# Where the two parts of each matmul operand lie in SBUF: offsets and shared tiles in a two-layer decoder trunk

## Chip, core and metric

The kernel runs on one core of a Trainium2 chip. The metric is the device time of one execution in microseconds (us). TensorE does the matrix products, VectorE (DVE) and ScalarE (ACT) the elementwise work, GpSimd (POOL) a few small things; SP issues nearly all DMAs. SBUF is the on-chip memory of 128 partitions; an "address" below is a byte offset inside a partition, the same for all of them. PSUM holds the sums of the matmuls.

## The reference

Two layers over 256 tokens of width 1024, all in float32:

```
for l in range(2):
    x = x + 0.5 * swiglu(rmsnorm(x), ffn1_w_in[l], ffn1_w_out[l])      # 1024 -> 2 x 2816 -> 1024
    h = rmsnorm(x)
    hq, hf, hi, hg, aq, ak, av, ga, gb = split(h @ w_in[l])            # 1024 -> 10752
    y_a = hgrn2(hq, hf, hi, hg) @ w_branch_a[l]                        # gated recurrence, 8 heads
    y_b = dilated_attention(aq, ak, av) @ w_branch_b[l]                # 3 groups of 4 heads, 512 -> 1024
    x = x + (sigmoid(ga) * y_a + sigmoid(gb) * y_b) @ w_out[l]
    x = x + 0.5 * swiglu(rmsnorm(x), ffn2_w_in[l], ffn2_w_out[l])
```

## The kernel before

**Precision.** Every float32 operand of the big products is split into two float32r parts: "hi", a rounded copy, and "lo", the rest. A product is then three matmuls: hi x hi, hi x lo and lo x hi. For weights ACT makes hi (a Copy, L195 or L241) and DVE makes lo (a subtraction, L196 or L242). Activations are split in the same way where they are made: `xh`/`xl` (the normed x, in `norm_parts`), `hh`/`hl` (the hidden layer of SwiGLU), `ph`/`pl` (first the recurrence's output `oah`/`oal`, later the merged branches `mgh`/`mgl`, both in the same two buffers), and `obh`/`obl` (the attention's output). Each of these eight is a tile of its own before the change.

**Two forms of product.** A matmul has a standing operand (128 columns, loaded into the array by a weight load ahead of it) and a moving operand (streamed through).

- `full` and `mm_feat` (L209 to L211): the weights stand, 256 tokens of activations move. Used for both halves of SwiGLU's first product, for SwiGLU's second product except the very last one, for hf, hq, the gates, and the products with w_branch_a, w_branch_b and w_out.
- `wide` and `mm_half` (L219 to L221): 128 tokens of activations stand, 512 columns of weights move. Used for hi, hg, aq, ak, av and for the last product of the kernel, which writes the output.

The three matmuls of the first form, for each row tile k of 128 rows and each 128 columns of weights:

```
nc.tensor.matmul(o, hi[:, f], ah[:, k0 + k, :], start=s, ...)
nc.tensor.matmul(o, hi[:, f], al[:, k0 + k, :], ...)
nc.tensor.matmul(o, lo[:, f], ah[:, k0 + k, :], ..., stop=e)
```

In the profile `mm<-xh,whi` names the output tile, then the inputs.

**Weights.** A unit is up to eight row tiles of 256 columns (1 MB). SP loads it into one of three `raw` buffers; ACT and DVE convert it in half units of four row tiles into `whi` and `wlo`, four buffers each. ACT and DVE work their queues in order, so a conversion that waits for a free buffer holds up what is queued behind it there.

**Addresses.** The tile framework lays out its pools one after the other: the constants (with `xT`, `xh`, `xl`), then `wts` (`raw`, `whi`, `wlo`), and behind it the pools that come and go: `ffn` with `hh`/`hl`; `mix` with `ph`/`pl` and `mg`, and inside it `hgrn` or `attn`. Sizes are rounded to 32 bytes. One row tile of a weight part takes 1024 bytes in a partition, so does one row tile of an activation part, and a step of 128 columns is 512 bytes.

**Order.** The order of instructions on each engine is planned by the framework from the program's order, the tiles' dependences and a model of time (`schedule_with_timeline_sim=True`). It fills the recurrence's and the attention's small float32 matmuls in between the large products. No order is written out by hand around the change, except for `HEAD_ORDER` inside the attention.

Of the kernel before, what the change touches and what calls it, by code (L numbers as in the profile page):

```python
# [31 lines left out]
HEADS = 8  # L32
EPS = 1e-6
# [4 lines left out]
# columns of the constant table  # L38
# [9 lines left out]
def _shape_constants():  # L48
    """Identity, rotary tables and 0/1 or additive masks: functions of the shapes alone."""
    c = np.zeros((128, C_END), np.float32)  # L50
    c[:, C_ID:C_ID + 128] = np.eye(128, dtype=np.float32)
    inv = (10000.0 ** (-np.arange(0, 128, 2) / 128.0)).astype(np.float32)
    ang = np.arange(T, dtype=np.float32)[:, None] * inv[None, :]
    cos, sin = np.cos(ang.astype(np.float64)), np.sin(ang.astype(np.float64))
    for h in range(2):
        r = slice(h * 128, (h + 1) * 128)
        c[:, C_COS + h * 128:C_COS + (h + 1) * 128] = np.concatenate([cos[r], cos[r]], 1)
        c[:, C_SIN + h * 128:C_SIN + (h + 1) * 128] = np.concatenate([-sin[r], sin[r]], 1)
    for h, base, n in ((0, C_M0, 128), (1, C_M1, 256)):
        t = np.arange(128)[:, None] + 128 * h  # L60
        s = np.arange(n)[None, :]
        for g, (w, d) in enumerate(((128, 1), (512, 4), (2048, 16))):
            ok = (t - s >= 0) & (t - s <= w) & ((t - s) % d == 0)
            c[:, base + g * n:base + (g + 1) * n] = np.where(ok, 0.0, -BIG)
    s = (np.arange(128) % 32)[:, None]
    t = np.arange(32)[None, :]
    lv = [(s // 4 == t // 4) & (t - s == d) for d in range(4)]
    lv += [(s // 16 == t // 16) & (t // 4 - s // 4 == d) for d in range(1, 4)]
    lv += [(s < 16) & (t >= 16)]
    for i, m in enumerate(lv):  # L70
        c[:, C_LV + i * 32:C_LV + (i + 1) * 32] = m
    return c
# [3 lines left out]
def trunk(ctx, tc, x, ffn1_norm, ffn1_w_in, ffn1_w_out, mix_norm, w_in, lb_logits, out_norm,  # L76
# [13 lines left out]
    xT = const.tile([128, KD, T], F32, name="xT")  # L90
    xh = const.tile([128, KD, T], F32R, name="xh")
    xl = const.tile([128, KD, T], F32R, name="xl")
# [90 lines left out]
    def unit(w, r0, nk, col, step=0):  # L183
        raw = wts.tile([128, KD, CU], F32, name="raw", bufs=RB)
        for a in range(0, nk, step or nk):
            n = min(step or nk, nk - a)
            nc.sync.dma_start(raw[:, a:a + n, :], w[r0 + a * 128:r0 + (a + n) * 128, col:col + CU].rearrange(
                "(k p) c -> p k c", p=128))
        parts = []
        for a in range(0, nk, step or KH):  # L190
            n = min(step or KH, nk - a)
            hi = wts.tile([128, KH, CU], F32R, name="whi", bufs=WB)
            lo = wts.tile([128, KH, CU], F32R, name="wlo", bufs=WB)
            r = raw[:, a:a + n, :]
            nc.scalar.activation(hi[:, :n, :], r, AF.Copy)  # L195
            nc.vector.tensor_sub(lo[:, :n, :], r, hi[:, :n, :].bitcast(F32))  # L196
            parts += [(hi[:, k, :], lo[:, k, :]) for k in range(n)]
        return parts

    def mm_feat(ps, wu, ah, al, k0, nk, first, last):  # L200
        """ps[feature, fb, token] += W^T a"""
        for k in range(nk):
            hi, lo = wu[k]
            for fb in range(2):
# [3 lines left out]
                e = last and k == nk - 1  # L208
                nc.tensor.matmul(o, hi[:, f], ah[:, k0 + k, :], start=s, stop=False, skip_group_check=True)  # L209
                nc.tensor.matmul(o, hi[:, f], al[:, k0 + k, :], start=False, stop=False, skip_group_check=True)  # L210
                nc.tensor.matmul(o, lo[:, f], ah[:, k0 + k, :], start=False, stop=e, skip_group_check=True)  # L211

    def mm_half(o, h, wu, ah, al, k0, nk, first, last):
        """o[token of half h, column] += a^T W"""
# [8 lines left out]
    def full(w, col, ah, al, nk=KD, step=0):  # L223
        wu = unit(w, 0, nk, col, step)
        ps = ps_mm.tile([128, 512], F32, name="mm")
        mm_feat(ps, wu, ah, al, 0, nk, True, True)
        return ps

    def wide(w, col, ah, al, nk=KD):
        """ps[half][token, column] = a^T W for 512 columns"""  # L230
        ps = [ps_mm.tile([128, 512], F32, name="mm") for _ in range(2)]
        for k0 in range(0, nk, 4):
# [4 lines left out]
            for a in range(0, n, 2):  # L237
                hi = wts.tile([128, KH, CU], F32R, name="whi", bufs=WB).rearrange("p (k a) c -> p k (a c)", a=2)
                lo = wts.tile([128, KH, CU], F32R, name="wlo", bufs=WB).rearrange("p (k a) c -> p k (a c)", a=2)
# [52 lines left out]
    def ffn(l, gi, w1, w2, to_out, x0=None):  # L292
        norm_parts(gi, l)
        with ExitStack() as es:
            fp = es.enter_context(tc.tile_pool(name="ffn", bufs=2))
            hh = fp.tile([128, KF, T], F32R, name="hh", bufs=1)
            hl = fp.tile([128, KF, T], F32R, name="hl", bufs=1)
            xt = None
            for j in range(DFF // CU):
                pa = full(w1, j * CU, xh, xl, step=0 if j or l or gi else FIRST)  # L300
# [8 lines left out]
                pb = full(w1, DFF + j * CU, xh, xl)  # L309
# [15 lines left out]
            if to_out:  # L325
                for c in range(D // CW):
                    ps = wide(w2, c * CW, hh, hl, KF)
# [5 lines left out]
            else:  # L333
                for c in range(D // CU):
                    ps = ps_mm.tile([128, 512], F32, name="mm")
                    k0 = 0
                    for nk in (8, 8, 6):
                        wu = unit(w2, k0 * 128, nk, c * CU)
                        mm_feat(ps, wu, hh, hl, k0, nk, k0 == 0, k0 + nk == KF)
# [5 lines left out]
    def hgrn_pair(wp, st, l, u, pf, vg):  # L345
        W, X, ATs = st
        w = w_in[l]
        if pf is None:
            pf = full(w, MIX_HF + u * CU, xh, xl)
# [9 lines left out]
        pq = full(w, MIX_HQ + u * CU, xh, xl)  # L359
# [8 lines left out]
        if u % 2 == 0:  # L368
            pv = wide(w, MIX_HI + u * CU, xh, xl)
# [8 lines left out]
        def variants(Y, s0, B, m):  # L378
            """Y slot s0 holds queries decayed to the start of their m-block; the next slots
            carry them over one, two and three more m-blocks of the same 4m-block."""  # L380
# [6 lines left out]
        def suffix(B, m, kin, name):  # L387
            """products behind each m-block inside its 4m-block, and the keys carried to its end"""
# [13 lines left out]
        def diag(Y, s0, m, dst):  # L402
            """queries decayed to the start of their 4m-block: slot j for the m-block j"""
# [48 lines left out]
        def carry(m, B, last=False):  # L452
            """queries and keys from blocks of m to blocks of 2m"""
# [37 lines left out]
        if u % 2:  # L491
            pg = wide(w, MIX_HG + (u - 1) * CU, xh, xl)
# [40 lines left out]
    def attn(ap, l, obh, obl):  # L533
# [5 lines left out]
        def qk_unit(i, base, dst, g):  # L539
# [6 lines left out]
            ps = wide(w, base + g * CW, xh, xl)  # L546
# [30 lines left out]
        def v_unit(g):  # L577
            ps = wide(w, MIX_AV + g * CW, xh, xl)
# [54 lines left out]
    def mix(l):  # L633
        norm_parts(1, l)
        with ExitStack() as es:
            mp = es.enter_context(tc.tile_pool(name="mix", bufs=1))
            pf0 = full(w_in[l], MIX_HF, xh, xl)
            with tc.tile_pool(name="norm", bufs=2) as work:
                norm_scale(work, square_sums(work))
            oah = mp.tile([128, KD, T], F32R, name="ph", tag="ph", bufs=1)  # L640
            oal = mp.tile([128, KD, T], F32R, name="pl", tag="pl", bufs=1)
# [16 lines left out]
            def gate(base, u, dst):  # L658
                ps = full(w, base + u * CU, xh, xl)
# [5 lines left out]
            with ExitStack() as e2:  # L665
                ap = e2.enter_context(tc.tile_pool(name="attn", bufs=1))
                obh = ap.tile([128, 4, T], F32R, name="obh")
                obl = ap.tile([128, 4, T], F32R, name="obl")
                attn(ap, l, obh, obl)
                if l == 0:  # L670
                    lower_bounds()
                for u in range(D // CU):
                    ps = full(w_a[l], u * CU, oah, oal)
                    s = slice(2 * u, 2 * u + 2)
                    nc.vector.tensor_mul(mg[:, s, :], mg[:, s, :], v2(ps))
                mgh = mp.tile([128, KD, T], F32R, name="ph", tag="ph", bufs=1)
                mgl = mp.tile([128, KD, T], F32R, name="pl", tag="pl", bufs=1)
                gb = {}

                def branch_b(u):  # L680
                    ps = full(w_b[l], u * CU, obh, obl, nk=4)
# [14 lines left out]
            for u in range(D // CU):  # L696
                ps = full(w_out[l], u * CU, mgh, mgl)
# [33 lines left out]
```

## Time and profile before

| what | value |
|---|---|
| time of three runs | 1459.36, 1459.47, 1461.06 us; median 1459.47 |
| profiled execution: span from first to last instruction | 1458.1 us |
| TensorE busy (matmuls) | 1448.9 us, 99%, 11362 matmuls |
| weight loads busy | 1366.3 us, 94% |
| DVE busy | 996.0 us, 68% |
| ACT busy | 791.1 us, 54% |
| HBM traffic | 172 GB/s over the span |

The profiled execution's own time is known by its span; a run's time has what lies around the span in addition, and the three runs lie 1.3 to 3.0 us above it. The "busy" time of TensorE is a union of intervals whose ends are modelled: matmuls overlap, and a row's mean length is not the distance from one matmul to the next. That distance ("step" below) is read from the start times of successive rows in the timeline, or from the count of matmuls in a window that holds only one kind.

### The profile page before, as it was taken

What the parts mean: (1) busy time and instruction counts of PE and PEld (TensorE: products, weight loads), DVE (VectorE), ACT (ScalarE), POOL (GpSimd) and SP (SyncE); (2) the same over time, 40 slices, a digit from 0 to 9 for tenths busy, and PEclk for the clock granted to TensorE, in tenths of its full rate; (3) what the DMA queues carried; (4) which work ended last, traced back from release to release, by engine and by line L of the source; (5) the groups of instructions that cost most, each with busy time, mean ns of one, the idle gap of its engine ahead of it and who ended that gap; (6) DMA issues with size and microseconds to landing.
All of it is one profiled execution on the core that took longest, in us unless ns stands there. A gap on an engine that the chain in (4) does not pass through costs nothing.

```text
span 1458.1 us, 26998 instructions
## 1 busy us (share of the span) xinstructions
PE 1448.9 (99%) x11362; PEld 1366.3 (94%) x11362; DVE 996.0 (68%) x1452; ACT 791.1 (54%) x1259; POOL 91.3 (6%) x86
## 2 busy tenths in 40 slices
PE   8999999999999999999999999999999999999999
PEld 8999998898889999999999999988988899999987
DVE  6666559776976586665566655698779766766653
ACT  6544447667864555444444444566577646554432
POOL 0000010002510000000000000100034000000000
PEclk9999999999999999999999999999999999999999
DMA  9565564345554365555555555544454534555552
GB/s 309 176 195 177 178 203 156 135 145 174 173 174 146 115 202 176 196 178 186 190 174 190 186 164 189 197 147 144 149 173 171 179 125 138 195 186 191 174 187 101
DMA packets 215881, 253.17 MB, mean 174 GB/s; under 512 B 4224, under 2 KB 182608, under 8 KB 215760
## 3 DMA queue, kind: packets, MB, share of 16 engines
q1 hardware_dynamic: 215584, 251.38, 51.8%
q8 instruction: 89, 1.46, 0.4%
q14 instruction: 32, 0.26, 0.1%
q10 hardware_dynamic: 176, 0.07, 0.0%
HBM read 250.39 MB, written 1.05 MB: 172 GB/s over the span
## 4 chain that ended last, share of the span: by engine, by line
PE 99%; DMA 0%; ACT 0%; SPq 0%; DVE 0%; issue 0%; ACTq 0%
PE mm L209 23%; PE mm L211 23%; PE mm L210 23%; PE mm L221 8%; PE mm L219 8%; PE mm L220 8%; PE sm L415 1%; PE sm L595 1%; PE tr L574 1%; PE sm L614 1%; PE sm L606 1%; PE sm L616 0%; DMA x<-in_x_dram 0%; PE sm L480 0%; PE sm L525 0%; PE sm L506 0%
## 5 line engine op out<-in xcount | busy, mean ns | idle before, releaser
L195 ACT ACTIVATE whi<-raw 128x1024 fp32r<-128x1024 f32 (+1 forms) x354 | 367.9, 1041 | 435.4 <-PE mm L210 339.8
L196 DVE TENSOR_TENSOR wlo<-raw,whi 128x1024 fp32r<-128x1024 f32 (+1 forms) x354 | 424.2, 1199 | 244.3 <-ACT whi L195 242.6
L209 PE MATMUL mm<-xh,whi 128*128 128x256 f32 x1920 | 540.7, 282 | 1.4 <-ACT whi L195 1.4
L211 PE MATMUL mm<-xh,wlo 128*128 128x256 f32 x1920 | 540.9, 282 | 0.0
L210 PE MATMUL mm<-xl,whi 128*128 128x256 f32 x1920 | 539.4, 281 | 0.0
L209 PEld LDWEIGHTS mm<-xh,whi 128*128 128x128 f32 x1920 | 362.6, 189 | 2.8 <-ACT whi L195 1.8
L211 PEld LDWEIGHTS mm<-xh,wlo 128*128 128x128 f32 x1920 | 362.5, 189 | 1.2 <-issue 0.4
L210 PEld LDWEIGHTS mm<-xl,whi 128*128 128x128 f32 x1920 | 362.4, 189 | 0.6
L242 DVE TENSOR_TENSOR wlo<-raw,whi 128x1024 fp32r<-128x1024 f32 x126 | 155.2, 1233 | 62.5 <-ACT whi L241 62.2
L241 ACT ACTIVATE whi<-raw 128x1024 fp32r<-128x1024 f32 x126 | 132.6, 1060 | 98.0 <-PE mm L221 53.1
L219 PE MATMUL mm<-whi,xh 128*128 128x512 f32 x416 | 166.7, 401 | 0.0
L221 PE MATMUL mm<-whi,xl 128*128 128x512 f32 x416 | 165.8, 399 | 0.0
L220 PE MATMUL mm<-wlo,xh 128*128 128x512 f32 x416 | 164.8, 396 | 0.0
L211 PE MATMUL mm<-hh,wlo 128*128 128x256 f32 x528 | 149.5, 283 | 0.0
L210 PE MATMUL mm<-hl,whi 128*128 128x256 f32 x528 | 149.5, 283 | 0.0
L209 PE MATMUL mm<-hh,whi 128*128 128x256 f32 x528 | 149.4, 283 | 0.0
L210 PEld LDWEIGHTS mm<-hl,whi 128*128 128x128 f32 x528 | 100.8, 191 | 0.0
L211 PEld LDWEIGHTS mm<-hh,wlo 128*128 128x128 f32 x528 | 100.8, 191 | 0.0
L209 PEld LDWEIGHTS mm<-hh,whi 128*128 128x128 f32 x528 | 100.8, 191 | 0.0
L221 PEld LDWEIGHTS mm<-whi,xl 128*128 128x128 f32 x416 | 78.1, 188 | 18.4
L220 PEld LDWEIGHTS mm<-wlo,xh 128*128 128x128 f32 x416 | 78.2, 188 | 17.7
L219 PEld LDWEIGHTS mm<-whi,xh 128*128 128x128 f32 x416 | 78.2, 188 | 16.9
(194 smaller groups left out, 1753.2 us busy)
## 6 DMA issues: line engine op xcount, KB each, us to landing
raw<-in_ffn_w_in_dram SPq DMA_DIRECT2D x87, 1024.0 KB, 5.1
raw<-in_w_in_dram SPq DMA_DIRECT2D x84, 1024.0 KB, 4.9
raw<-in_ffn_w_out_dram SPq DMA_DIRECT2D x34, 1024.0 KB, 5.1
raw<-in_ffn_w_out_dram SPq DMA_DIRECT2D x12, 768.0 KB, 4.4
raw<-in_w_branch_a_dram SPq DMA_DIRECT2D x8, 1024.0 KB, 5.1
raw<-in_w_out_dram SPq DMA_DIRECT2D x8, 1024.0 KB, 5.4
raw<-in_w_branch_b_dram SPq DMA_DIRECT2D x8, 512.0 KB, 3.4
x<-in_x_dram SPq DMA_DIRECT2D x4, 256.0 KB, 4.0
```

The lines of the kernel that those rows point to most:

```text
L195: nc.scalar.activation(hi[:, :n, :], r, AF.Copy)
L196: nc.vector.tensor_sub(lo[:, :n, :], r, hi[:, :n, :].bitcast(F32))
L209: nc.tensor.matmul(o, hi[:, f], ah[:, k0 + k, :], start=s, stop=False, skip_group_check=True)
L210: nc.tensor.matmul(o, hi[:, f], al[:, k0 + k, :], start=False, stop=False, skip_group_check=True)
L211: nc.tensor.matmul(o, lo[:, f], ah[:, k0 + k, :], start=False, stop=e, skip_group_check=True)
L219: nc.tensor.matmul(o, ah[:, k0 + k, t], hi, start=s, stop=False, skip_group_check=True)
L220: nc.tensor.matmul(o, ah[:, k0 + k, t], lo, start=False, stop=False, skip_group_check=True)
L221: nc.tensor.matmul(o, al[:, k0 + k, t], hi, start=False, stop=e, skip_group_check=True)
L241: nc.scalar.activation(hi, r, AF.Copy)
L242: nc.vector.tensor_sub(lo, r, hi.bitcast(F32))
L415: nc.tensor.matmul(p[32 * b:32 * b + 32, c * n:(c + 1) * n], kk[:, o], mov(o), start=True, stop=True, tile_position=(0, 32 * b))
L574: nc.tensor.transpose(pt[:, h, c * 128:(c + 1) * 128], z[:, c, 2 * a + h, :], ident)
```

## The change

Three things, on addresses alone:

- The hi and lo parts of one operand become two views of one tile. For activations (`parts_of`) the parts alternate row tile by row tile: hi of row tile 0, lo of row tile 0, hi of row tile 1, and so on, 1024 bytes each. For weights (`weight_parts`) hi is the first half and lo the second.
- The views begin at a chosen offset inside the tile: 128 bytes for `xp` (formerly `xh`, `xl`), 32 for `hp` and `pp`, 0 for `obp`; 0 for weights used as the standing operand, 32 for weights used as the moving one. The padding behind keeps sizes as they are needed for the next tile's address: a multiple of 512 for `xp` and the weight tiles.
- `mm_feat` marks only the last matmul of a product as the end of its group, where before the last one of each half was marked.

Buffer counts, instruction counts, loads and the order in the program stay. The diff, without the renamed arguments and dropped comments:

```diff
+LINE = 512
+STEP = 32
...
+    def parts_of(pool, n, name, at=STEP, pad=STEP):
+        t = pool.tile([128, n * 2 * T + pad // 4], F32R, name=name, bufs=1)
+        return t[:, at // 4:at // 4 + n * 2 * T].rearrange("p (k a t) -> p k a t", a=2, t=T)
+
+    def weight_parts(at, c):
+        n = KH * CU
+        t = wts.tile([128, 2 * n + LINE // 4], F32R, name="wp", bufs=WB)
+        return [t[:, at // 4 + i * n:at // 4 + (i + 1) * n].rearrange("p (k c) -> p k c", c=c) for i in range(2)]
+
+    def halves(p):
+        return p[:, :, 0, :], p[:, :, 1, :]
...
-    xh = const.tile([128, KD, T], F32R, name="xh")
-    xl = const.tile([128, KD, T], F32R, name="xl")
+    xp = parts_of(const, KD, "xp", 128, LINE)
+    xh, xl = halves(xp)
...
     def unit(w, r0, nk, col, step=0):
...
-            hi = wts.tile([128, KH, CU], F32R, name="whi", bufs=WB)
-            lo = wts.tile([128, KH, CU], F32R, name="wlo", bufs=WB)
+            hi, lo = weight_parts(0, CU)
...
-    def mm_feat(ps, wu, ah, al, k0, nk, first, last):
+    def mm_feat(ps, wu, ap, k0, nk, first, last):
         for k in range(nk):
             hi, lo = wu[k]
+            ah, al = (ap[:, k0 + k, i, :] for i in range(2))
             for fb in range(2):
...
-                e = last and k == nk - 1
+                e = last and k == nk - 1 and fb == 1
...
     def wide(...)
...
-                hi = wts.tile([128, KH, CU], F32R, name="whi", bufs=WB).rearrange("p (k a) c -> p k (a c)", a=2)
-                lo = wts.tile([128, KH, CU], F32R, name="wlo", bufs=WB).rearrange("p (k a) c -> p k (a c)", a=2)
+                hi, lo = weight_parts(STEP, CW)
...
-            hh = fp.tile([128, KF, T], F32R, name="hh", bufs=1)
-            hl = fp.tile([128, KF, T], F32R, name="hl", bufs=1)
+            hp = parts_of(fp, KF, "hp")
+            hh, hl = halves(hp)
...
-            oah = mp.tile([128, KD, T], F32R, name="ph", tag="ph", bufs=1)
-            oal = mp.tile([128, KD, T], F32R, name="pl", tag="pl", bufs=1)
+            oap = parts_of(mp, KD, "pp")
+            oah, oal = halves(oap)
...
-                obh = ap.tile([128, 4, T], F32R, name="obh")
-                obl = ap.tile([128, 4, T], F32R, name="obl")
-                attn(ap, l, obh, obl)
+                obp = parts_of(ap, 4, "obp", 0)
+                attn(ap, l, *halves(obp))
...
-                mgh = mp.tile([128, KD, T], F32R, name="ph", tag="ph", bufs=1)
-                mgl = mp.tile([128, KD, T], F32R, name="pl", tag="pl", bufs=1)
+                mgp = parts_of(mp, KD, "pp")
+                mgh, mgl = halves(mgp)
```

More of the change, by code (lines that the diff above doesn't have):

```diff
@@ L207, in mm_feat @@
                 s = first and k == 0 and fb == 0
-                e = last and k == nk - 1
-                nc.tensor.matmul(o, hi[:, f], ah[:, k0 + k, :], start=s, stop=False, skip_group_check=True)
-                nc.tensor.matmul(o, hi[:, f], al[:, k0 + k, :], start=False, stop=False, skip_group_check=True)
-                nc.tensor.matmul(o, lo[:, f], ah[:, k0 + k, :], start=False, stop=e, skip_group_check=True)
+                e = last and k == nk - 1 and fb == 1
+                nc.tensor.matmul(o, hi[:, f], ah, start=s, stop=False, skip_group_check=True)
+                nc.tensor.matmul(o, hi[:, f], al, start=False, stop=False, skip_group_check=True)
+                nc.tensor.matmul(o, lo[:, f], ah, start=False, stop=e, skip_group_check=True)
     def mm_half(o, h, wu, ah, al, k0, nk, first, last):
@@ L221, in mm_half, with full, wide @@
             nc.tensor.matmul(o, al[:, k0 + k, t], hi, start=False, stop=e, skip_group_check=True)
-    def full(w, col, ah, al, nk=KD, step=0):
+    def full(w, col, ap, nk=KD, step=0):
         wu = unit(w, 0, nk, col, step)
         ps = ps_mm.tile([128, 512], F32, name="mm")
-        mm_feat(ps, wu, ah, al, 0, nk, True, True)
+        mm_feat(ps, wu, ap, 0, nk, True, True)
         return ps
-    def wide(w, col, ah, al, nk=KD):
+    def wide(w, col, ap, nk=KD):
+        ah, al = halves(ap)
         ps = [ps_mm.tile([128, 512], F32, name="mm") for _ in range(2)]
@@ L295, in ffn @@
             fp = es.enter_context(tc.tile_pool(name="ffn", bufs=2))
-            hh = fp.tile([128, KF, T], F32R, name="hh", bufs=1)
-            hl = fp.tile([128, KF, T], F32R, name="hl", bufs=1)
+            hp = parts_of(fp, KF, "hp")
+            hh, hl = halves(hp)
             xt = None
             for j in range(DFF // CU):
-                pa = full(w1, j * CU, xh, xl, step=0 if j or l or gi else FIRST)
+                pa = full(w1, j * CU, xp, step=0 if j or l or gi else FIRST)
                 if j == 0:
@@ L308, in ffn @@
                 nc.scalar.activation(a, a, AF.Silu)
-                pb = full(w1, DFF + j * CU, xh, xl)
+                pb = full(w1, DFF + j * CU, xp)
                 b = fp.tile([128, 2, T], F32, name="fb")
@@ L326, in ffn @@
                 for c in range(D // CW):
-                    ps = wide(w2, c * CW, hh, hl, KF)
+                    ps = wide(w2, c * CW, hp, KF)
                     for h in range(2):
@@ L338, in ffn @@
                         wu = unit(w2, k0 * 128, nk, c * CU)
-                        mm_feat(ps, wu, hh, hl, k0, nk, k0 == 0, k0 + nk == KF)
+                        mm_feat(ps, wu, hp, k0, nk, k0 == 0, k0 + nk == KF)
                         k0 += nk
@@ L348, in hgrn_pair @@
         if pf is None:
-            pf = full(w, MIX_HF + u * CU, xh, xl)
+            pf = full(w, MIX_HF + u * CU, xp)
         f = wp.tile([128, 2, T], F32, name="hf", bufs=2)
@@ L358, in hgrn_pair @@
         nc.scalar.activation(k, f, AF.Copy, scale=-1.0, bias=1.0)
-        pq = full(w, MIX_HQ + u * CU, xh, xl)
+        pq = full(w, MIX_HQ + u * CU, xp)
         z = wp.tile([128, 2, T], F32, name="hz", bufs=1)
@@ L368, in hgrn_pair @@
         if u % 2 == 0:
-            pv = wide(w, MIX_HI + u * CU, xh, xl)
+            pv = wide(w, MIX_HI + u * CU, xp)
             vg["v"] = wp.tile([128, 2, CW], F32, name="hv", bufs=1)
@@ L491, in hgrn_pair @@
         if u % 2:
-            pg = wide(w, MIX_HG + (u - 1) * CU, xh, xl)
+            pg = wide(w, MIX_HG + (u - 1) * CU, xp)
             vg["g"] = wp.tile([128, 2, CW], F32, name="hgs", bufs=1)
@@ L545, in qk_unit @@
             nc.gpsimd.tensor_mul(gs[:, :, 64:128], sin_t[:, :, 64:128], gr[:, None, 0:64].to_broadcast([128, 2, 64]))
-            ps = wide(w, base + g * CW, xh, xl)
+            ps = wide(w, base + g * CW, xp)
             z = ap.tile([128, 2, 4, 128], F32, name="az", bufs=2)
@@ L577, in v_unit @@
         def v_unit(g):
-            ps = wide(w, MIX_AV + g * CW, xh, xl)
+            ps = wide(w, MIX_AV + g * CW, xp)
             for c in range(2):
@@ L636, in mix @@
             mp = es.enter_context(tc.tile_pool(name="mix", bufs=1))
-            pf0 = full(w_in[l], MIX_HF, xh, xl)
+            pf0 = full(w_in[l], MIX_HF, xp)
             with tc.tile_pool(name="norm", bufs=2) as work:
                 norm_scale(work, square_sums(work))
-            oah = mp.tile([128, KD, T], F32R, name="ph", tag="ph", bufs=1)
-            oal = mp.tile([128, KD, T], F32R, name="pl", tag="pl", bufs=1)
+            oap = parts_of(mp, KD, "pp")
+            oah, oal = halves(oap)
             mg = mp.tile([128, KD, T], F32, name="mg", bufs=1)
@@ L658, in gate @@
             def gate(base, u, dst):
-                ps = full(w, base + u * CU, xh, xl)
+                ps = full(w, base + u * CU, xp)
                 nc.vector.tensor_mul(dst, v2(ps), Rb2)
@@ L672, in mix @@
                 for u in range(D // CU):
-                    ps = full(w_a[l], u * CU, oah, oal)
+                    ps = full(w_a[l], u * CU, oap)
                     s = slice(2 * u, 2 * u + 2)
                     nc.vector.tensor_mul(mg[:, s, :], mg[:, s, :], v2(ps))
-                mgh = mp.tile([128, KD, T], F32R, name="ph", tag="ph", bufs=1)
-                mgl = mp.tile([128, KD, T], F32R, name="pl", tag="pl", bufs=1)
+                mgp = parts_of(mp, KD, "pp")
+                mgh, mgl = halves(mgp)
                 gb = {}
                 def branch_b(u):
-                    ps = full(w_b[l], u * CU, obh, obl, nk=4)
+                    ps = full(w_b[l], u * CU, obp, nk=4)
                     s = slice(2 * u, 2 * u + 2)
@@ L696, in mix @@
             for u in range(D // CU):
-                ps = full(w_out[l], u * CU, mgh, mgl)
+                ps = full(w_out[l], u * CU, mgp)
                 xs = xT[:, 2 * u:2 * u + 2, :]
```

## The prediction, made before the changed kernel had run

> **What bounds the kernel now.** I read the page first (busy shares, granted clock, chain), then the waits of TensorE, then its groups of instructions, then windows of single stages and the start times in them.
>
> ```profile
> span 1458.1 us, 26998 instructions
> PE 1448.9 (99%) x11362; PEld 1366.3 (94%) x11362; DVE 996.0 (68%) x1452; ACT 791.1 (54%) x1259; POOL 91.3 (6%) x86
> PEclk9999999999999999999999999999999999999999
> ...
> PE 99%; DMA 0%; ACT 0%; SPq 0%; DVE 0%; issue 0%; ACTq 0%
> PE mm L209 23%; PE mm L211 23%; PE mm L210 23%; PE mm L221 8%; PE mm L219 8%; PE mm L220 8%; PE sm L415 1%; PE sm L595 1%; PE tr L574 1%; PE sm L614 1%; PE sm L606 1%; PE sm L616 0%; DMA x<-in_x_dram 0%; PE sm L480 0%; PE sm L525 0%; PE sm L506 0%
> ...
> L195 ACT ACTIVATE whi<-raw 128x1024 fp32r<-128x1024 f32 (+1 forms) x354 | 367.9, 1041 | 435.4 <-PE mm L210 339.8
> L196 DVE TENSOR_TENSOR wlo<-raw,whi 128x1024 fp32r<-128x1024 f32 (+1 forms) x354 | 424.2, 1199 | 244.3 <-ACT whi L195 242.6
> ```
> ```profile
> PE sm L148 <- DMA x<-in_x_dram: 4.2, 2, 3.9
> PE mm L209 <- ACT whi L195: 1.4, 1, 1.4
> ```
>
> The chain is TensorE for 99%, the granted clock is at 90% or more in every slice (1.00 in the windows below), and TensorE waits twice on the first input and once (1.4 us) on a weight conversion. After the start nothing is late for it: the time is the sum of the start-to-start distances (steps) of its matmuls, 93% of it on the six lines L209 to L221. A faster step is worth its full size, and nothing else is worth anything. The matmuls overlap, so the "mean ns of one" is not the step; that has to come from start times. The groups give the counts (L209, L210 and L211 have the same counts among themselves, so have L219, L220 and L221):
>
> ```profile
> L209 PE MATMUL mm<-xh,whi 128*128 128x256 f32 x1920 | 540.7, 282 | 1.4 <-ACT whi L195 1.4
> L219 PE MATMUL mm<-whi,xh 128*128 128x512 f32 x416 | 166.7, 401 | 0.0
> L209 PE MATMUL mm<-hh,whi 128*128 128x256 f32 x528 | 149.4, 283 | 0.0
> L209 PE MATMUL mm<-ph,whi 128*128 128x256 f32 x256 | 71.6, 283 | 0.0
> L219 PE MATMUL mm<-whi,hh 128*128 128x512 f32 x88 | 34.3, 390 | 0.0
> L209 PE MATMUL mm<-obh,whi 128*128 128x256 f32 x64 | 18.2, 285 | 0.0
> ```
>
> I call "narrow" the matmuls with standing weights (256 moving columns of activations) and "wide" those with standing activations (512 moving columns of weights). Narrow: 3 x 1920 = 5760 on x, and 3 x (528 + 256 + 64) = 2544 on the other activations. Wide: 3 x 416 = 1248 on x, 3 x 88 = 264 on hh.
>
> Now the steps. Windows of stages with nothing but narrow matmuls (on x, hh, x, hh, ph), with the first and last starts of three of them:
>
> ```profile
> 40.00:100.00 60.00, 60.00 (x513) 60.00 (x512) 40.10 (x43) 29.87 (x33) 0.00 (x0) 1.00 0.59 192
> 140.00:199.00 59.00, 59.00 (x495) 59.00 (x493) 28.93 (x32) 24.36 (x29) 0.00 (x0) 1.00 0.56 183
> 600.00:660.00 60.00, 60.00 (x508) 60.00 (x507) 39.86 (x43) 28.05 (x31) 0.00 (x0) 1.00 0.58 192
> 673.00:730.00 57.00, 57.00 (x477) 57.00 (x476) 28.99 (x33) 25.70 (x31) 0.00 (x0) 1.00 0.57 190
> 523.00:542.00 19.00, 19.00 (x160) 19.00 (x159) 13.74 (x20) 11.34 (x17) 0.00 (x0) 1.00 0.51 167
> 1270.00:1390.00 120.00, 120.00 (x1014) 120.00 (x1013) 79.17 (x87) 57.66 (x65) 1.72 (x1) 1.00 0.56 185
> ```
> ```profile
> 40.05 0.28 PE L209 MATMUL mm<-xh,whi 128*128 128x256 f32 x1
> ...
> 99.89 0.28 PE L209 MATMUL mm<-xh,whi 128*128 128x256 f32 x1
> ...
> 140.08 0.28 PE L209 MATMUL mm<-hh,whi 128*128 128x256 f32 x1
> ...
> 199.00 0.28 PE L211 MATMUL mm<-hh,wlo 128*128 128x256 f32 x1
> ...
> 600.03 0.28 PE L211 MATMUL mm<-xh,wlo 128*128 128x256 f32 x1
> ...
> 659.96 0.28 PE L209 MATMUL mm<-xh,whi 128*128 128x256 f32 x1
> ```
>
> Two or three of each count began before the window. So 40 to 100 holds 511 starts: (99.89 - 40.05) / 510 = 117.3 ns on x. On hh it is 58.92 us / 491 = 120.0 ns. In the next x stage 59.93 / 505 = 118.7 ns. The other rows agree: 57 / 475 = 120.0 on hh, 19 / 158 = 120.3 on ph (a short window, so its edges count), 120 / 1012 = 118.6 on x. One shape, one clock, 56 to 59% DMA share in the long windows, and yet x is always 1.3 to 2.7 ns quicker than hh.
>
> The wide ones, on x in attention and on hh at the end: the first and the last of 19 and of 13 starts, and a weight load:
>
> ```profile
> 344.19 0.39 PE L221 MATMUL mm<-whi,xl 128*128 128x512 f32 x1
> ...
> 348.39 0.39 PE L221 MATMUL mm<-whi,xl 128*128 128x512 f32 x1
> ```
> ```profile
> 344.20 0.19 PEld L219 LDWEIGHTS mm<-whi,xh 128*128 128x128 f32 x1
> ```
> ```profile
> 1420.07 0.39 PE L221 MATMUL mm<-whi,hl 128*128 128x512 f32 x1
> ...
> 1422.79 0.39 PE L221 MATMUL mm<-whi,hl 128*128 128x512 f32 x1
> ```
>
> 4.20 / 18 = 233.3 ns on x, 2.72 / 12 = 226.7 ns on hh: again one shape and two steps. The load row (344.20) stands beside the matmul before it (344.19): while one matmul reads its moving operand, the next one's standing operand is read.
>
> **What differs is the address.** From the allocation table of the compiled kernel before: xh lies at byte 24704 of each partition, xl at 32896, whi from 83168, wlo from 99552, hh and ph at 115936, obh at 140512. Modulo 512, xh and xl are at 128 and everything else (hl, pl, obl too) at 224. Inside a tile all operands move by multiples of 512 bytes, so this holds for every matmul. Narrow on x: standing weights 96 above the moving activations modulo 512, which is 32 below modulo 128: 117.3 to 118.7 ns. Narrow on hh, ph, ob: level, 120.0. Wide on x: standing activations 96 below the moving weights: 233.3. Wide on hh: level, 226.7. So the trace of before holds both relations of both kinds, bar one detail below.
>
> **The change, part by part.** Where things land: xp begins where xh did and its data 128 bytes in (24832, 256 modulo 512); it is 512 bytes longer than xh and xl, so the weights start at 83680, still 224. One wp tile is 8192 + 512 = 8704 bytes, 17 x 512, so all four stand at 224; narrow weights begin there, wide ones 32 bytes in, at 256. The pools behind begin at 118496 (224); hp and pp start 32 in (256), and obp, behind pp's 16416 and mg's 8192 bytes, at 143104 (256). Every narrow matmul then has standing weights 32 below the moving activations, every wide one is level.
>
> 1. Wide on x goes from the 233.3 relation to the 226.7 one: 1248 x 6.6 ns = 8.2 us less. Ends: 0 (the two stages differ for another reason) and 8.2.
> 2. Narrow on hh, ph and ob goes from 120.0 to x's step. That is 117.3 in the first of four long x stages and 118.6 in the others, mean 118.3: 2544 x 1.7 = 4.3 us less. Ends: 2544 x 1.3 = 3.3 and 2544 x 2.7 = 6.9, and 0 for the reason above.
> 3. Narrow on x keeps its place modulo 128 but goes from +96 to -32 modulo 512; no row shows -32. Same step taken, 0, because the same 32-byte distance modulo 128 is the nearest row. Ends: all in the quick state, 5760 x 1.0 = 5.8 us less; or as dear as the level relation, 5760 x 1.7 = 9.8 us more.
> 4. Wide on hh stays level (both 256 instead of both 224): 0.
> 5. Hi and lo share a tile: ACT's conversion into a freed tile waits for the last L211 instead of the last L210, one step (0.12 us) later. A half unit is 24 steps, 2.8 us, and with four tiles three half units (8.5 us) lie ahead of TensorE when ACT starts; ACT and DVE need 1.04 + 1.20 us. ACT's 339.8 us of waiting for L210 are that lead. Behind the waiting ACT conversion stand its DVE half and ACT's own next steps, which have the same slack: 0. No instruction and no DMA is added or removed; the stop flag sits on one matmul fewer per product: 0.
> 6. The fp32 matmuls and transposes are the other 7% of the chain, about 100 us. They keep their distances inside a pool and shift 32 or 64 bytes against the identity. No row prices this; by the only relation on show (233.3 / 226.7, 2.9%) it is at most 3 us either way. Taken 0, since most of them have both operands in one pool.
> 7. The order of instructions is planned anew. TensorE waits for nothing, so order is worth only its switches between kinds:
>
> ```profile
> 261.70 0.28 PE L209 MATMUL mm<-xh,whi 128*128 128x256 f32 x1
> 261.82 0.28 PE L210 MATMUL mm<-xl,whi 128*128 128x256 f32 x1
> 262.03 0.68 PE L480 MATMUL sm<-hqq,s4k 128*64 128x64 f32 x8
> 262.64 0.39 PE L211 MATMUL mm<-xh,wlo 128*128 128x256 f32 x1
> 262.87 0.28 PE L209 MATMUL mm<-xh,whi 128*128 128x256 f32 x1
> ```
>
> The steps at 261.82 and 262.64 are 0.21 and 0.23 us instead of 0.12: 0.2 us for a visit. Ten visits more or fewer would be 2 us; taken 0, because the tiles keep their number and order.
>
> Sum: 8.2 + 4.3 = 12.5 us, span 1458.1 to 1445.6. The median of the runs (1459.47) is 1.4 us above the span, so 1447.0 us (-0.86%).
>
> The trace prices the two relations of one wide shape at 233.3 and 226.7 ns. The Trainium skill, SBUF — State Buffer, section "Who interferes with whom", says the opposite: TensorE's moving operand and its weight load have a read port each, independent of each other, and TensorE never waits on anyone. By that rule addresses could not matter and the sum would be 0 instead of 12.5 us; the trace disagrees as far as its two groups differ by address alone.
>
> **The rivals.**
> - No effect: the steps differ through their stages (other DVE and ACT work, data), not the address. For it: the address relation and the stage go together in this trace, and x itself has two steps (117.3, 118.7) at one relation. Against: hh shows 120.0 in two different feed-forward parts and ph about 120 in the mixer, with different DVE and ACT loads. Time 1459.5. It is what the skill page's rule gives.
> - Only the wide part works: 1459.5 - 8.2 = 1451.3. Only the narrow part: 1455.2.
> - Slower: -32 modulo 512 is a bad place for narrow matmuls, unlike +96. All 8304 narrow matmuls now stand there, so it is dear. Price by the only bad relation on show, 233.3 / 226.7 = 1.029 over level: 120.0 x 1.029 = 123.5 ns, 5760 x 5.2 + 2544 x 3.5 - 8.2 us = +30.7 us, 1490. It decides from a mean narrow step of 119.8 ns on (8304 steps then eat the 8.2 us). Between, with all narrow matmuls at 120.0: 9.8 - 8.2 = +1.6 us, 1461.1.
> - The shared tile exposes conversions: the short products on obh have four row tiles each, where the lead is thinnest, eight tiles in all, 1.0 us if the 0.12 us of each were exposed: 1448. Only if no lead is left anywhere would all 354 conversions of L195 cost it, 42 us, 1489. The 8.5 us of lead and the single wait of TensorE speak against it.
>
> **How the numbers follow.** Both parts as summed 0.60; only wide 0.08; only narrow 0.06; no effect 0.10; narrow dearer 0.10 (half near 1461, half well above); exposed waits or a worse order 0.06, of which half still come out under 1456. What a measurement of this kernel tells from no change is 0.2%, 2.9 us: faster means under 1456.6. Faster 0.60 + 0.08 + 0.06 + 0.03 = 0.77; same 0.10 + 0.03 + 0.02 = 0.15; slower 0.08. The likeliest case alone spans 1459.5 - 8.2 - 6.9 - 5.8 = 1438.6 to 1459.5 - 8.2 - 3.3 = 1448.0, a little more if narrow on x settles on 118.7 everywhere (2.3 us): 1450. The range takes in the one-part cases and no effect: 1438 to 1460.
>
> **What would show it.** Right: windows of wide matmuls on x step at 226 to 227 ns, the windows on hp, pp and obp at 117 to 119, those on xp in narrow form unchanged at 117 to 119, TensorE still 99% of the chain with no new wait. Step 1 is wrong if wide on xp stays above 230; step 2 if hp stays at 120.0; step 3 if narrow on xp leaves 117.3 to 118.7; step 5 if the waits of TensorE on the conversions exceed 1.4 us in total. The prediction as a whole fails if narrow steps on x rise past 119.8 ns.

## The result and the profile after

The changed kernel takes 1437.66 us (median of 5 runs, 1437.16 to 1437.82) against 1460.74 us for the kernel before on the same chip: ratio 0.9842, 95% interval 0.983 to 0.9854. That is 23 us or 1.6% less, nearly twice the 12.5 us forecast. The profiled execution has a span of 1435.4 us and a time of 1437.16 us.

From the page of the changed kernel, busy shares and chain, then (from its waits) what TensorE waited for:

```profile
span 1435.4 us, 26973 instructions
PE 1426.2 (99%) x11362; PEld 1351.5 (94%) x11362; DVE 994.5 (69%) x1452; ACT 791.0 (55%) x1259; POOL 92.5 (6%) x86
...
PE 99%; ACT 0%; DMA 0%; DVE 0%; issue 0%
...
L211 ACT ACTIVATE wp<-raw 128x1024 fp32r<-128x1024 f32 (+1 forms) x354 | 367.9, 1040 | 424.0 <-PE mm L228 332.8
```
```profile
PE sm L165 <- DMA x<-in_x_dram: 3.9, 1, 3.9
PE mm L226 <- ACT wp L211: 1.5, 1, 1.5
```

The picture is the old one: as many matmuls, TensorE the whole chain, no new wait. ACT now waits for L228 (the last of the three matmuls) instead of L210, which costs TensorE nothing. So the gain is all in the steps. Below are windows of the changed kernel on xp, hp, xp, hp, pp and xp. They hold narrow matmuls alone, except that the third and the last have a handful of others. The columns are the stretch, then busy time and count of TensorE, of the weight loads, DVE, ACT and POOL, the clock and DMA. The step is the window plus one duration (0.28 us), divided by the first count:

```profile
40.00:100.00 60.00, 60.00 (x517) 60.00 (x516) 40.49 (x43) 29.88 (x33) 0.00 (x0) 1.00 0.59 192
140.00:196.00 56.00, 56.00 (x483) 56.00 (x482) 28.22 (x31) 24.02 (x28) 0.00 (x0) 1.00 0.60 193
540.00:600.00 60.00, 60.00 (x517) 60.00 (x516) 40.22 (x46) 29.69 (x33) 1.52 (x1) 1.00 0.59 192
662.00:720.00 58.00, 58.00 (x499) 58.00 (x498) 30.95 (x35) 25.71 (x32) 0.00 (x0) 1.00 0.58 187
514.00:535.00 21.00, 21.00 (x180) 21.00 (x180) 15.88 (x23) 12.59 (x19) 0.00 (x0) 1.00 0.52 165
1250.00:1368.00 118.00, 118.00 (x1014) 118.00 (x1013) 78.49 (x86) 57.42 (x65) 1.52 (x1) 1.00 0.57 188
```

That is 116.6 ns on xp, 116.5 and 116.8 on hp, 118.2 on pp, 116.6 again on xp at the end. (In the short window on pp one matmul counts 0.7 ns; the mean over the stage's 192 start times is 117.8.) Both kinds have left the steps they had before: hh stood at 120.0, and x at 117.3 in its first long stage and 118.7 in the others.

The wide steps in the timeline, on xp (first and last of 16 starts):

```profile
340.25 0.39 PE L236 MATMUL mm<-wp,xp 128*128 128x512 f32 x1
...
343.65 0.39 PE L236 MATMUL mm<-wp,xp 128*128 128x512 f32 x1
```

3.40 us / 15 = 226.7 ns, the step that only hh had before.

Adding up all times from one start to the next, by the kind of the earlier matmul, shows where the 22.7 us of span went (differences are of the unrounded sums):

| kind | before, us | after, us | difference | forecast |
|---|---|---|---|---|
| narrow on x (5760) | 689.7 | 682.9 | -6.8 | 0 |
| narrow on hh, ph, ob (2544) | 306.7 | 299.2 | -7.4 | -4.3 |
| wide on x (1248) | 296.2 | 289.3 | -6.9 | -8.2 |
| wide on hh (264) | 59.9 | 59.9 | 0 | 0 |
| fp32 matmuls and transposes | 97.7 | 96.1 | -1.6 | 0 |

### The profile page after: what moved, and what is told of

It is laid out like the page before. It is cut to its first block, busy times and chain, and to the rows that moved or that the text cites. A ratio compares the mean times of both kernels' runs of the same rounds, so it can differ in the third digit from the quotient of the medians.

```text
span 1435.4 us, 26973 instructions
## 1 busy us (share of the span) xinstructions
PE 1426.2 (99%) x11362; PEld 1351.5 (94%) x11362; DVE 994.5 (69%) x1452; ACT 791.0 (55%) x1259; POOL 92.5 (6%) x86
## 4 chain that ended last, share of the span: by engine, by line
PE 99%; ACT 0%; DMA 0%; DVE 0%; issue 0%
PE mm L226 23%; PE mm L228 23%; PE mm L227 23%; PE mm L236 8%; PE mm L238 8%; PE mm L237 8%; PE sm L432 1%; PE sm L612 1%; PE tr L591 1%; PE sm L631 1%; PE sm L623 1%; PE sm L633 0%; PE sm L497 0%; PE sm L542 0%; PE sm L523 0%; PE sm L524 0%
## 5 line engine op out<-in xcount | busy, mean ns | idle before, releaser
L211 ACT ACTIVATE wp<-raw 128x1024 fp32r<-128x1024 f32 (+1 forms) x354 | 367.9, 1040 | 424.0 <-PE mm L228 332.8
L212 DVE TENSOR_TENSOR wp<-raw,wp 128x1024 fp32r<-128x1024 f32 (+1 forms) x354 | 424.1, 1199 | 244.8 <-ACT wp L211 243.3
L226 PE MATMUL mm<-xp,wp 128*128 128x256 f32 x1920 | 538.4, 281 | 1.5 <-ACT wp L211 1.5
L228 PE MATMUL mm<-xp,wp 128*128 128x256 f32 x1920 | 538.7, 281 | 0.0
L227 PE MATMUL mm<-xp,wp 128*128 128x256 f32 x1920 | 538.3, 281 | 0.0
L226 PEld LDWEIGHTS mm<-xp,wp 128*128 128x128 f32 x1920 | 361.8, 189 | 3.1 <-ACT wp L211 1.9
L228 PEld LDWEIGHTS mm<-xp,wp 128*128 128x128 f32 x1920 | 361.8, 189 | 0.9 <-DVE wp L212 0.2
L227 PEld LDWEIGHTS mm<-xp,wp 128*128 128x128 f32 x1920 | 362.0, 189 | 0.6
L259 DVE TENSOR_TENSOR wp<-raw,wp 128x1024 fp32r<-128x1024 f32 x126 | 155.9, 1237 | 64.8 <-ACT wp L258 64.3
L258 ACT ACTIVATE wp<-raw 128x1024 fp32r<-128x1024 f32 x126 | 133.1, 1063 | 82.9 <-PE mm L238 46.2
L236 PE MATMUL mm<-wp,xp 128*128 128x512 f32 x416 | 164.7, 396 | 0.0
L238 PE MATMUL mm<-wp,xp 128*128 128x512 f32 x416 | 163.6, 393 | 0.0
L237 PE MATMUL mm<-wp,xp 128*128 128x512 f32 x416 | 162.8, 391 | 0.0
L227 PE MATMUL mm<-hp,wp 128*128 128x256 f32 x528 | 147.3, 279 | 0.0
L228 PE MATMUL mm<-hp,wp 128*128 128x256 f32 x528 | 147.3, 279 | 0.0
L226 PE MATMUL mm<-hp,wp 128*128 128x256 f32 x528 | 147.3, 279 | 0.0
L226 PEld LDWEIGHTS mm<-hp,wp 128*128 128x128 f32 x528 | 99.2, 188 | 0.0
L227 PEld LDWEIGHTS mm<-hp,wp 128*128 128x128 f32 x528 | 99.2, 188 | 0.0
L228 PEld LDWEIGHTS mm<-hp,wp 128*128 128x128 f32 x528 | 99.2, 188 | 0.0
L238 PEld LDWEIGHTS mm<-wp,xp 128*128 128x128 f32 x416 | 78.1, 188 | 16.1
L237 PEld LDWEIGHTS mm<-wp,xp 128*128 128x128 f32 x416 | 78.2, 188 | 15.4
L236 PEld LDWEIGHTS mm<-wp,xp 128*128 128x128 f32 x416 | 78.2, 188 | 15.3
```

The lines of the kernel that those rows point to most:

```text
L226: nc.tensor.matmul(o, hi[:, f], ah, start=s, stop=False, skip_group_check=True)
L227: nc.tensor.matmul(o, hi[:, f], al, start=False, stop=False, skip_group_check=True)
L228: nc.tensor.matmul(o, lo[:, f], ah, start=False, stop=e, skip_group_check=True)
L236: nc.tensor.matmul(o, ah[:, k0 + k, t], hi, start=s, stop=False, skip_group_check=True)
L237: nc.tensor.matmul(o, ah[:, k0 + k, t], lo, start=False, stop=False, skip_group_check=True)
L238: nc.tensor.matmul(o, al[:, k0 + k, t], hi, start=False, stop=e, skip_group_check=True)
```

## The experiments

Theory R: the step is set by the distance in bytes, modulo some power of two, from the operand that is moving to the standing operand of the next matmul, which is read at the same time. (That it is the next one's and not its own no run here can tell, because both have the same address modulo 512.) Rival S: the gain comes from the sharing of tiles, hi and lo of a row tile now lying next to each other. The first four runs change one thing each.

**Offsets without sharing of the activations' tiles.**

```diff
-        t = pool.tile([128, n * 2 * T + pad // 4], F32R, name=name, bufs=1)
+        h = pool.tile([128, n * T + pad // 4], F32R, name=name + "h", bufs=1)
+        lo = pool.tile([128, n * T + (pad if pad == LINE else 0) // 4], F32R, name=name + "l", bufs=1)
...
```

> The changed kernel with hi and lo of every activation in tiles of their own again (weights still share a tile), at the same places modulo 512 as in the changed kernel (256 for activations, 224 for narrow and 256 for wide weights). Theory R (the step is set by the distance between the moving operand and the next standing one, modulo 512: -32 is a better place than +96): narrow steps stay at 116.7 ns, 1437 to 1439 us. Rival S (the quicker narrow step comes from hi and lo alternating in one tile, 1 KB apart, and -32 and +96 are the same place modulo 128): narrow on x goes back to 118.2, the rest too, 8304 x 1.5 ns = 12 us more, about 1450.

Measured: 1436.57 us, ratio to before 0.9833 (0.9818 to 0.9847).

```profile
40.00:100.00 60.00, 60.00 (x516) 60.00 (x516) 40.01 (x43) 29.95 (x34) 0.00 (x0) 1.00 0.58 191
514.00:535.00 21.00, 21.00 (x183) 21.00 (x182) 16.02 (x23) 11.95 (x18) 0.00 (x0) 1.00 0.51 163
```

516 starts in 60.28 us are 116.8 ns, as with shared tiles. On pp it is 21.28 / 183 = 116.3 (116.7 by the start times), a little quicker than above. S falls for the activations: with the offsets in place, sharing their tiles adds nothing.

**Sharing without offsets.**

```diff
-LINE = 512
-STEP = 32
+LINE = 0
+STEP = 0
...
-    xp = parts_of(const, KD, "xp", 128, LINE)
+    xp = parts_of(const, KD, "xp", 0, 0)
```

> Sharing alone: the parts share tiles as in the changed kernel, but with no offsets, so that every operand stands modulo 512 where it stood before the change (x at 128, all else at 224, narrow and wide). Theory R: the steps of before come back, 118.2 on x, 120.0 on the other narrow ones, 233.4 wide on x: 1459 to 1461 us. Rival S: narrow on x keeps 116.8, about 8 us under the kernel before, 1452; the wide part goes back to 233.4 under both.

Measured: 1455.42 us, ratio 0.9967 (0.9954 to 0.9979). That is below R's 1459 and above S's 1452, so neither theory had the time. Windows on x, x and hp:

```profile
40.00:100.00 60.00, 60.00 (x513) 60.00 (x512) 40.22 (x43) 29.85 (x33) 0.00 (x0) 1.00 0.59 192
545.00:600.00 55.00, 55.00 (x471) 55.00 (x471) 36.58 (x43) 26.95 (x30) 1.52 (x1) 1.00 0.58 185
675.00:730.00 55.00, 55.00 (x461) 55.00 (x460) 28.08 (x32) 24.65 (x30) 0.00 (x0) 1.00 0.55 177
```

On hp 55.28 / 461 = 119.9 ns, and wide on x stays at 233.4: the steps of before, as R says. On x it is 117.5 and 117.4. The 117.3 of the first x stage before the change now holds in all four, where three stood at 118.7. By the sums of steps, narrow on x is 3.6 us less than before the change and the fp32 work 1.1 us less. So there is a gain of 5 us that distances don't explain: at one and the same distance a stage can settle on one of two steps. This run has the new order and the moved stop flag as well as the shared tiles, so which of the three brought it stays open. The runs at 64 bytes, below, come back to the two steps.

**The wide offset taken back.**

```diff
-                hi, lo = weight_parts(STEP, CW)
+                hi, lo = weight_parts(0, CW)
```

> The changed kernel with the 32 bytes ahead of the wide products' weights taken out: moving weights stand 32 below the standing activations instead of level with them; narrow as changed. Theory R: wide on x goes from 227.9 ns back to about 233 (the distance is the old one modulo 128) and wide on hh too: 1248 x 5.5 + 264 x 6.4 = 8.5 us more, 1446. Rival (the wide gain comes from the shared tile or the new order): no change, 1437.7.

Measured: 1445.55 us, ratio 0.9894 (0.9879 to 0.9909), 7.9 us above the changed kernel; expected was 1446 by R. Timeline of wide on xp, first and last of 22 starts:

```profile
344.22 0.40 PE L236 MATMUL mm<-wp,xp 128*128 128x512 f32 x1
...
349.12 0.40 PE L236 MATMUL mm<-wp,xp 128*128 128x512 f32 x1
```

4.90 us / 21 = 233.3 ns. Wide on hp is level in both kernels and is taken 32 bytes off here. First and last of 13 of its starts:

```profile
1409.61 0.40 PE L236 MATMUL mm<-wp,hp 128*128 128x512 f32 x1
...
1412.41 0.40 PE L236 MATMUL mm<-wp,hp 128*128 128x512 f32 x1
```

2.80 us / 12 = 233.3 ns, and over the whole stage the mean went from 227.0 to 233.3: the same stage with the same neighbours, only the address moved. That answers the doubt behind the "no effect" rival.

**x alone taken back to 128 modulo 512.**

```diff
-    xp = parts_of(const, KD, "xp", 128, LINE)
+    xp = parts_of(const, KD, "xp", 0, LINE)
```

> The changed kernel with x alone moved 128 bytes down, to 128 modulo 512 as before: narrow on x has its standing weights 96 above the moving operand instead of 32 below (the same modulo 128), wide on x has its moving weights 128 above the standing operand (level modulo 128). Theory R with modulo 512: narrow on x goes back to 118.2, 5760 x 1.4 = 8 us more, and if wide needs level modulo 512 too, 7 us on top: 1446 or 1453. Theory R with modulo 128 alone, and S: nothing changes, 1437.7.

Measured: 1447.69 us, ratio 0.9909 (0.9894 to 0.9923), 10.0 us above the changed kernel. Windows of narrow on x, and wide on x (first and last of 22 starts):

```profile
40.00:100.00 60.00, 60.00 (x514) 60.00 (x512) 39.89 (x43) 30.15 (x34) 0.00 (x0) 1.00 0.60 194
1260.00:1370.00 110.00, 110.00 (x940) 110.00 (x939) 72.77 (x80) 53.00 (x59) 1.52 (x1) 1.00 0.58 189
```
```profile
344.02 0.40 PE L236 MATMUL mm<-wp,xp 128*128 128x512 f32 x1
...
348.90 0.40 PE L236 MATMUL mm<-wp,xp 128*128 128x512 f32 x1
```

Narrow on x is back at 60.28 / 514 = 117.3 and 110.28 / 940 = 117.3, 5.2 us more over the kernel. Three of its four long stages stand there; the third stands at 118.8, so here too one distance has two steps. Wide on x is at 4.88 / 21 = 232.4 although it is level modulo 128, 5.5 us more. So 128 is not the period, for either kind: +96 is not -32, and +128 is not level.

**Which period, and which distance is best.** One run with another offset for every product:

```diff
-            hi, lo = weight_parts(0, CU)
+            at = (16 * (7 * turn[0] % 32) + 32) % 512     # turn[0] counts the calls
+            hi, lo = weight_parts(at, CU)
...
-                hi, lo = weight_parts(STEP, CW)
+                hi, lo = weight_parts(at, CW)             # at runs over 28 other multiples of 16
```

> The changed kernel with another offset of the weight tile's views for each product: narrow standing weights stand r = 0, 16, ... 496 bytes above the moving activations modulo 512 (about 5 products of up to 48 matmuls each per value, mixed in order), wide moving weights w = 16 times n above the standing activations (every multiple of 16 but -32, 0, 96 and 128, one product each). Theory R: steps depend on r and w, with r = 480 near 116.7 ns, r = 96 at 117.3 to 118.7, r = 0 at 120.0, each repeated at every product with the same r. If only the distance modulo 128 counted, values 128 apart would have equal steps. Open, and no theory says: whether a place below 116.7 or below 226.7 exists. Rival (the stage or the order sets the step): all r alike, 116.7 to 120.

Measured: 1456.3 us in one run. Two products from its timeline, at r = 320 and at r = 256. Each has 48 starts, of which the first and the last are shown:

```profile
82.06 0.28 PE L233 MATMUL mm<-xp,wp 128*128 128x256 f32 x1
...
87.40 0.28 PE L232 MATMUL mm<-xp,wp 128*128 128x256 f32 x1
...
104.62 0.28 PE L233 MATMUL mm<-xp,wp 128*128 128x256 f32 x1
...
110.26 0.28 PE L232 MATMUL mm<-xp,wp 128*128 128x256 f32 x1
```

5.34 / 47 = 113.6 ns and 5.64 / 47 = 120.0 ns, 17 us apart in the same stage. The tables have mean steps over all products with the same distance, for a good half of the values of r and a third of those of w: r for narrow (some 170 to 290 steps each), w for wide (some 45 each, some 130 at w = 160 and 336, where the last products fell).

| r | 0 | 32 | 64 | 96 | 128 | 160 | 192 | 208 | 224 |
|---|---|---|---|---|---|---|---|---|---|
| step at r, ns | 119.7 | 118.4 | 114.1 | 118.6 | 119.5 | 119.8 | 117.8 | 117.0 | 117.1 |
| step at r + 256, ns | 120.0 | 118.4 | 113.7 | 118.2 | 119.2 | 119.6 | 117.8 | 116.8 | 117.5 |

| w | 16 | 64 | 112 | 160 | 176 | 192 | 224 | 240 | 256 |
|---|---|---|---|---|---|---|---|---|---|
| step, ns | 231.8 | 229.6 | 231.4 | 234.2 | 233.3 | 233.3 | 233.5 | 234.0 | 227.5 |

The period is 256 bytes: values 256 apart agree within 0.4 ns, values 128 apart differ by up to 3.7 (64 and 192). It is the distance that counts and not one operand's address alone: level gives 120 ns with both operands at 224 (before the change) and with both at 256 (here). -32 is 480, the +96 of before is 96. Between them lies 1 ns, and the best narrow place, 64, is one that neither kernel uses. For wide the next best after level (227.5 at 256) is 229.6, at 64.

**64 above instead of 32 below**, with the changed kernel again beside it:

```diff
-            hi, lo = weight_parts(0, CU)
+            hi, lo = weight_parts(96, CU)
```

> The changed kernel with one number altered: the narrow weights begin 96 instead of 0 bytes into their tile, so they stand 64 above the moving activations modulo 512 instead of 32 below. Theory R by the scan (r = 64 at 114.1 ns and r = 320 at 113.7 including the ends of the products, 113 or 114 in most steps): 8304 narrow steps x (116.8 - 113.5) = 27 us less than the changed kernel, 1410 us. Rival (the quick step is a state that only short runs between other distances show): as the changed kernel, 1437 us.

> The changed kernel once more, as the measure for the run with 64 above on the same chip: 1437 to 1438 us under every theory.

Measured: 1430.29 us, ratio 0.9799 (0.9778 to 0.9821); the changed kernel beside it 1437.26 us, 0.9838 (0.9822 to 0.9855). The gain is 7 us instead of the expected 27. Three of the four runs took 1429.6 to 1430.7 us and one 1436.75: the same program doesn't always settle on the same steps, as far as the time alone can tell (that run has no trace). Windows of the run at 64, on xp, hp, xp, hp:

```profile
40.00:100.00 60.00, 60.00 (x532) 60.00 (x531) 40.74 (x44) 30.94 (x34) 0.00 (x0) 1.00 0.60 194
140.00:190.00 50.00, 50.00 (x444) 50.00 (x443) 26.26 (x29) 22.05 (x26) 0.00 (x0) 1.00 0.62 201
540.00:600.00 60.00, 60.00 (x512) 60.00 (x511) 41.38 (x46) 30.75 (x35) 0.00 (x0) 1.00 0.58 189
655.00:714.00 59.00, 59.00 (x503) 59.00 (x502) 30.90 (x35) 25.93 (x33) 0.00 (x0) 1.00 0.56 183
```

The first feed-forward stands at 113.3 and 113.2 ns, the second at 117.7 and 117.9, with one distance and one code. What the sharing run hinted at is plain here: a distance has several steady steps. The timeline shows where the second feed-forward takes the slower one, in its second product:

```profile
534.28 0.28 PE L228 MATMUL mm<-xp,wp 128*128 128x256 f32 x1
...
536.21 0.28 PE L226 MATMUL mm<-xp,wp 128*128 128x256 f32 x1
536.33 0.28 PE L227 MATMUL mm<-xp,wp 128*128 128x256 f32 x1
536.44 0.50 PE L287 MATMUL tr<-ones,nacc 128*128 128x1 f32 x4
536.80 0.36 PE L228 MATMUL mm<-xp,wp 128*128 128x256 f32 x1
537.00 0.28 PE L226 MATMUL mm<-xp,wp 128*128 128x256 f32 x1
...
540.65 0.28 PE L227 MATMUL mm<-xp,wp 128*128 128x256 f32 x1
```

Up to 536.21 the step is 1.93 / 17 = 113.5 ns, from 537.00 on 3.65 / 31 = 117.7. Between them lie four small fp32 matmuls of the norm (`tr`). In this trace, as in that of the changed kernel, each of the seven long narrow stretches without such an interruption keeps one step from end to end; every change of step between them falls at an interruption.

**A finer scan**, at multiples of 4 bytes:

```diff
-            at = (16 * (7 * turn[0] % 32) + 32) % 512
+            at = (fine[20 * turn[0] % 49] + 32) % 512     # fine: 4, 8, 12, 20, ... 252, and 64
```

> The scan again at multiples of 4 bytes that are not multiples of 16 (and r = 64): narrow r over 0 to 255, wide at 28 values around 0, 32, 188 and 250. Theory R, with lines of 16 bytes: a step depends on r only by the lines that both operands are in at a time, so values between two multiples of 16 lie between their steps, the best stays at r = 64 with 113.4 ns, and wide stays best at 0. Open: a place below 113.3 or 226.7 ns.

Measured: 1456.66 us in one run. Nothing is below 113.3 ns for narrow; r = 168 gave 113.3 over 180 steps with none above 115, r = 64 gave 113.4, r = 60 and 68 already 119.4 and 118.4. Wide is at 228.6 to 237.0 four bytes off level, and none of its 28 values reaches the 226.7 of level (the lowest is 227.9). That the values in between would lie between their neighbours was wrong: 168 lies between 160 (119.8) and 176 (118.1).

**168 above**, and behind it **64 above with another start.**

```diff
-            hi, lo = weight_parts(0, CU)
+            hi, lo = weight_parts(200, CU)
```

> The changed kernel with the narrow weights 200 bytes into their tile: 168 above the moving activations. In the fine scan this distance stood at 113.3 ns in all of its 180 steps, with none at 117 or 118, while 64 above has two states, 113.3 and 117.8, in the run at 64. If 168 has one state only: 8304 x (116.8 - 113.4) = 28 us less than the changed kernel, 1409 us. If it has a second state that four products were too few to show: between 1410 and 1437.

Measured: 1461.32 us, ratio to before 1.0003 (0.9994 to 1.0012). The whole gain is gone. Windows on xp:

```profile
40.00:100.00 60.00, 60.00 (x502) 60.00 (x502) 38.90 (x43) 29.53 (x33) 0.00 (x0) 1.00 0.59 192
545.00:600.00 55.00, 55.00 (x462) 55.00 (x461) 35.83 (x42) 26.52 (x29) 1.52 (x1) 1.00 0.57 180
```

120.1 and 119.7 ns: this distance has a second steady step too, which the four products of the scan had missed, and the kernel fell into it almost everywhere. In the scan each of the four followed a product at 64 that itself stood at 113.3 or 113.4.

Then 64 above again, with the products at the head of each half at 168 above:

```diff
+                place[0] = 96 if j else 200     # in the loop over w1; over w2: 96 if c else 200
-            hi, lo = weight_parts(96, CU)
+            hi, lo = weight_parts(place[0], CU)
```

> The run at 64 above with the first product of each feed-forward half at 168 above instead (the place with one state), the rest at 64. Theory H (at one distance the step has several steady states, and what ran just before chooses): the feed-forward stages that stood at 117.8 ns start from 113.3 and stay there, 3168 x 4.2 + 1056 x 4.4 = 18 us less than the run at 64, 1412 us. Rival (those stages are slower for where their buffers lie or what else runs there): only the products at 168 gain, some 3 us, 1427.

Measured: 1412.24 us, ratio to before 0.9669 (0.9656 to 0.9683). Windows as for the run at 64:

```profile
40.00:100.00 60.00, 60.00 (x531) 60.00 (x531) 40.75 (x44) 30.93 (x34) 0.00 (x0) 1.00 0.61 196
140.00:190.00 50.00, 50.00 (x444) 50.00 (x443) 25.96 (x29) 22.35 (x26) 0.00 (x0) 1.00 0.61 199
540.00:600.00 60.00, 60.00 (x531) 60.00 (x530) 43.21 (x48) 31.31 (x36) 0.00 (x0) 1.00 0.61 199
655.00:707.00 52.00, 52.00 (x462) 52.00 (x461) 28.38 (x32) 24.08 (x30) 0.00 (x0) 1.00 0.59 189
```

Now the second feed-forward is at 113.5 and 113.2 like the first. In a feed-forward's first half two products of 22 stand elsewhere, and the 20 behind them keep the quick step for over 100 us on end. Theory H's time holds to a microsecond (1412 expected), and its rival (1427) falls: buffers and neighbours are as in the run at 64, and the stages that were slow there are quick here. What runs at the head of a stretch changes its step. But it isn't simply the distance of the product before: in the first feed-forward the two products at 168 stood at 120.0 and the next one, at 64, at 117.8, and 113.3 came only behind the next interruption, as in the run at 64. In the second one the fp32 matmuls that had ended the quick step now fall among the products at 168, which return to 113.3 after them. This version beats both kernels, the changed one by 25 us.

## Why the prediction was wrong

The direction was right, and so was the core of the mechanism: the steps follow distances between addresses. The size was not: the steps gave 10 us more than forecast, and the measured time lies 0.3 us outside the range.

- Step 1 (wide on x to level) was right: 233.4 to 227.9 ns on the mean of successive steps, 6.9 us against 8.2. The 226.7 of the steady rows isn't kept through the fp32 work in between, so 1248 x 6.6 was a little too much. Taking the 32 bytes back gave 233.3 on x and on hp.
- Step 2 (other narrow) had the right sign and was sized from the wrong row. It took x's 118.3, the price of +96, as the price of -32; that place measured 116.7 on hp, so it brought 7.4 us instead of 4.3.
- Step 3 (narrow on x, 0) is the step that failed; it brought 6.8 us. "The same 32-byte distance modulo 128 is the nearest row" assumed a period of 128. The scan shows 256, and there +96 and -32 are two places. About half of the 6.8 is the place: at +96 without offsets, and with all long stages on the quicker 117.4, narrow on x took 3.2 us more than in the changed kernel. The other 3.6 us is the price of the slower step at +96 in three stages, which the run with sharing alone lost at the same distance. The step named that one as its lower end, 5.8, and the sum put it at nothing.
- Steps 4 and 5 held: hh's wide steps are at 59.9 us in both traces, and TensorE waited 1.5 us for a conversion against 1.4. Steps 6 and 7 brought 1.6 us instead of 0. The run with sharing alone had 1.1 of it, so most comes with the shared tiles, the stop flag or the order made anew, not with the offsets.
- Of the rivals, "no effect" is refuted by the wide steps on hp (227.0 and 233.3 in one stage). The Trainium skill, SBUF — State Buffer, "Who interferes with whom", gives TensorE two independent read ports. If nothing else set the step, every distance would be alike; the scan has 113.6 and 120.0 ns in one stage, 17 us apart. The measurement decides against that consequence; where in the chip the time goes, no run here shows.
- The trace of before did hold a warning: x at one distance had two steps, 117.3 and 118.7. The prediction averaged them over the stages. Read as two states of one distance, they would have said that a row of a steady stream prices a distance only up to its state, 1.4 ns x 8304 = 12 us of uncertainty, and the range would have had to reach lower.

Still open: what in the chip has the period of 256 bytes, why an interruption by fp32 matmuls leaves the stream now on one step and now on another, and why sharing alone put all long x stages of the old distance on 117.4.

## What to carry to other kernels

Where one engine is the whole chain, divide stretches of the trace by their counts for each kind of operand: steps that differ at one shape and one clock are worth their difference times the count, here 48 us of 1460 between the kernel before and the last run. A distance between two operands that is only known modulo some power of two is not a known distance: scan it in one run, product by product, before pricing it. And check a best value over whole stages, with the interruptions that the kernel has: 168 bytes looked best in 180 steps of a scan and was worth nothing over the kernel.

## What the runs showed of the hardware that was not expected

- The step of back-to-back float32r matmuls depends on the distance between the moving and the standing operands, with a period of 256 bytes: 113.3 to 120 ns at 256 columns, 226.7 to 234 ns at 512 columns, at multiples of 16 bytes.
- At one distance there are several steady steps: 113.3 and 117.8 ns at 64, 113.3 and 120.0 at 168, 117.3 and 118.7 at 96, 116.7 and 117.8 at -32. A stream keeps its step until other matmuls interrupt it, for 100 us and more; in the run at 64 four small fp32 matmuls turned 113.3 into 117.8. Another distance in the first products of each feed-forward half changed which one held, 18 us over this kernel.
- No steady step came below 113.3 ns at 256 columns. The Trainium skill, TensorE: Matmul & The Clock Gate, section "Back-to-back issue gap", gives N / 2.4 + 2.5 ns as the gap of an isolated warm matmul, an estimate of 109.2 ns for 256 columns; no run here shows that.
